# A hybrid decoder layer on one core: the first layer norm's weight on VectorE, its bias as a 49th extra row

## The chip, the cores and the metric

The kernel runs on one core of a Trainium2 chip. A core has TensorE (PE) for matrix products, VectorE (DVE), ScalarE (ACT) and GpSimd (POOL) for elementwise work, and SyncE (SP), whose queue issues the DMAs of this kernel. The time is that of one execution on the device in microseconds (us); of several executions the median is given. A profile is one further execution, taken with the hardware profiler.

## What is computed

One layer on 2048 prompt tokens, 16 meta tokens and 32 sample tokens (8 sequences of 4). The model width D is 1024. Each token is first layer-normed with a weight and a bias (`ln0_g`, `ln0_b`); the result is both what the projections read and the residual that comes back in the last layer norm.

```python
def layer_norm(x, g, b):
    mu = jnp.mean(xf, -1, keepdims=True)
    var = jnp.mean(jnp.square(xf - mu), -1, keepdims=True)
    return (xf - mu) * lax.rsqrt(var + LN_EPS) * g + b

hp = layer_norm(concat([meta, x_prompt]), ln0_g, ln0_b)
hs = layer_norm(x_sample, ln0_g, ln0_b)
mq, mk, mv, mo, mz, mi, mf, aq, ak, av, az = split_proj(hp @ w_in + b_in)
h_m, state = mlstm_prompt(mq, mk, mv, mi, mf)      # chunks of 128 tokens, one after the other
h_a = swa_prompt(aq, ak, av, sink)                 # window of 128 tokens, the meta tokens always seen
mix = concat([gated_norm(h_m, mo, mz), h_a * silu(az)]) @ w_out
y = layer_norm(2**0.25 * hp + mix, ln_g, ln_b)
```

`mq`, `mk`, `mv`, `mo` have 512 columns each, the gates `mi` and `mf` 4 each, `mz`, `aq` and `az` 512 each, `ak` and `av` 128 each. The sample tokens go through the same layer from cached state; states and key/value caches are outputs too.

## The kernel before

**Tiling.** The prompt is cut into 16 chunks of 128 tokens, one token to a partition. The 32 sample tokens and the 16 meta tokens are the 48 "extra rows" (`NE`), one tile `xe`.

**Precision.** A number is carried as two float16 parts, high and low. A projection of a chunk (`proj`, lines 292 to 297) is 24 matmuls of 128x128 by 128x512 into one PSUM tile `pj`: for each of eight slices of D the high part of x times the high and the low part of w (lines 294 and 295), then the low part of x times the high part of w (line 297). `prep` makes the two parts of a weight: it finds the largest absolute value (`all_max` brings it to all partitions with a matmul, line 135), derives a power of two from it, then scales and rounds on ACT (line 269) and takes the difference on DVE (line 272). The float32 weights come through staging buffers (`stg`, and `stage` in the pool of weights). The extra rows' projection `proj_e` holds the high parts of the 48 rows in partitions 0 to 47 and the low parts from 64 on, so that one pass of 16 matmuls (lines 303 and 304) does both; two DVE operations (lines 307 and 313) add them and the bias.

**Stage A** (`a_steps`) goes through the chunks in order, for q, k, v, o and the gates of the mLSTM. `norm_x` normalises a chunk: `bn_stats` on DVE, the power -0.5 on POOL (line 325), scale and shift by the row's own statistics on ACT (line 331), the multiplication by `gs` and the addition of `bs`, each in two halves, on POOL (lines 374 and 375). Then ACT writes the high part `hl[:, 0]` (line 390) and DVE the low part (line 391), a DMA transposes both to `xT`, and the normalised chunk and `xT` are stored to DRAM (`h_d`, `xT_d`) for stage B. `a_gate` computes the gates; `log_sigmoid_rows` (lines 465 to 477) is a chain of tiny operations, of 128 or 48 partitions by 4 elements, which ends in `Gf` and `Gi`; these are transposed on PE (lines 577 for the extra rows, 739 for chunks). `m_rows`, `m_weights`, `m_T`, `m_S`, `m_num`, `m_kv` are the recurrence (lines 746 to 749 the scans, 823 the state's update). v goes to `vaug`, two tiles, used in turn by even and odd chunks. A bias tile `bA[i]` is `b_in` on all partitions; the evictions of PSUM (lines 423 and 426) add it.

**The start.** The order there is written out. The first chunk is normalised on DVE as a whole (`ln0_first`), is transposed in float32 on PE to `xf`, and its gates, q and k are projected from the float32 weights (`proj32`, line 410: two matmul rows of the trace for each of the eight slices), so that they need not wait for `prep`. v and o of the first chunk take the float16 path, with the transposed `xT0`. Between them stand the projections of the extra rows (`qe`, `ge`, `ke`, `ve`, `oe`), stored to `e_d` for the decode work.

**Extra work.** Sample tokens' work and the preparation of stage B's weights (`jobs`) are steps that are taken in turn with those of `a_steps`.

**Stage B** goes through the chunks once more: aq, ak and av, az, mz, the windowed attention (`s_unit`, `s_pv`), then `b_out`: `o_load` brings the chunk back from `h_d` to a tile `z` of the tag `xs` (two buffers), `o_half` multiplies by `w_out` and adds to `z` (line 1318), and `final` is the last layer norm (lines 1143 to 1145: one pass on DVE, two on POOL).

**Order.** The program is traced in this order, and the tile framework's scheduler then lays down one order for each engine from priorities and a modelled time; each engine executes its own list in order. `dma` holds SP's DMAs behind an anchor. SP's queue is in order too: a DMA that waits for a tile holds those behind it.

## Time and profile before

| what | value |
|---|---|
| time, median of 3 runs | 1107.26 us (1106.24 to 1110.84) |
| the profiled execution | 1109.82 us |
| its span on the core | 1108.0 us |
| mean granted clock of TensorE | 0.976 |
| DVE busy | 771.8 us |
| ACT busy | 411.5 us |

The span is what the profile covers; the 1.8 us around it belong to the execution. "Busy" is the time in which an engine executes something, register, branch, semaphore and DMA-issuing instructions aside. In a table of groups each row has the line, engine, operation, out<-in with the tile names and shapes, the count, then busy us and mean ns of one, then the idle us of the engine just before them with what ended that idle time. In the order of time a row starts with the start and the length in us. In a list of waits, a row says which engine waited, at which tile and line, for what: us in total, times, the longest.

### The profile page before, as it was taken

Reading aid. Unit: us, or ns where it says so; the run is one execution under the profiler, and the core shown is the slowest. Engines: PE = TensorE matmul, PEld = TensorE weight load, DVE = VectorE, ACT = ScalarE, POOL = GpSimd, SP = SyncE. Lnnn points to the kernel's source line nnn. Section 1 sums busy time; section 2 is a strip of 40 time slices with the busy share of each in tenths; the row PEclk is TensorE's granted clock in tenths of the full one; section 3 lists DMA queues with packets and bytes.
Section 4 is the critical chain, followed back from the end, with each engine's and each line's share of the span. In section 5 each row is a group of like instructions: output and inputs, shape, how many; then the busy total and the mean of one; then the engine's idle time right before and its main releaser. Section 6 shows DMA issues by size and latency. Waiting matters only on the chain.

```text
span 1108.0 us, 17830 instructions
## 1 busy us (share of the span) xinstructions
PE 1037.6 (94%) x6471; PEld 576.3 (52%) x6471; DVE 771.8 (70%) x2164; ACT 411.5 (37%) x980; POOL 326.7 (29%) x334
## 2 busy tenths in 40 slices
PE   7569999999898989989999899999999999999996
PEld 3235565655555445546655455555555555555543
DVE  6799677776488798875646766656766565676674
ACT  5653222226134355422214433433443343344430
POOL 4134444323043032321102223333322333332322
PEclk9869999999999999989999999999999999999998
DMA  9735745354773878763296456455454545555442
GB/s 321 200 99 162 148 127 146 101 143 146 202 205 93 253 240 271 219 195 87 58 362 133 105 120 134 119 122 120 109 122 122 138 113 122 126 107 119 100 112 74
DMA packets 246097, 166.03 MB, mean 150 GB/s; under 512 B 207977, under 2 KB 220985, under 8 KB 244441
## 3 DMA queue, kind: packets, MB, share of 16 engines
q1 hardware_dynamic: 246010, 164.90, 57.3%
q8 instruction: 51, 0.84, 0.3%
q14 instruction: 36, 0.29, 0.1%
HBM read 70.32 MB, written 45.68 MB: 105 GB/s over the span
## 4 chain that ended last, share of the span: by engine, by line
PE 68%; DVE 12%; DMA 11%; issue 4%; ACT 2%; POOL 1%; SPq 1%; DVEq 0%; POOLq 0%; ACTq 0%
PE pj L1314 14%; PE pj L297 14%; PE pj L295 13%; PE pj L294 13%; DMA xT<-hl 4%; PE pt L1234 2%; DMA xs<-in_dram 2%; PE po L1287 2%; DMA stg<-hl 2%; DMA stg<-in_dram 1%; PE pt L758 1%; DVE hl L391 1%; PE po L822 1%; DVE ls L473 1%; PE pj L410 1%
## 5 line engine op out<-in xcount | busy, mean ns | idle before, releaser
L1314 PE MATMUL pj<-wr_o,EE 128*128 128x512 f16 x720 | 167.1, 381 | 2.7 <-DMA EE<-stg 2.4
L295 PEld LDWEIGHTS <-xT 128*128 128x128 f16 x1008 | 99.2, 98 | 99.2 <-issue 6.1
L297 PEld LDWEIGHTS <-xT 128*128 128x128 f16 x1008 | 98.4, 98 | 98.2 <-issue 0.3
L294 PEld LDWEIGHTS <-xT 128*128 128x128 f16 x1008 | 99.4, 99 | 95.6 <-issue 3.6
L1314 PEld LDWEIGHTS <-EE 128*128 128x128 f16 x720 | 70.5, 98 | 79.8 <-DMA EE<-stg 3.3
L1247 POOL TENSOR_TENSOR mhl<-g,mhl 128x32 f16<-128x32 f32 x32 | 18.8, 587 | 144.6 <-ACT mhl L1246 140.2
L1247 POOL TENSOR_TENSOR mhl<-SI,mhl 128x32 f16<-128x32 f32 x32 | 19.0, 592 | 137.2 <-ACT mhl L1246 137.2
L1243 DVE TENSOR_TENSOR hl<-g,hl 128x512 f16<-128x512 f32 (+1 forms) x32 | 23.2, 724 | 40.7 <-ACT hl L1242 40.7
L294 PE MATMUL pj<-w_v,xT 128*128 128x512 f16 x128 | 50.1, 391 | 0.0
L295 PE MATMUL pj<-w_v,xT 128*128 128x512 f16 x128 | 49.7, 388 | 0.4 <-DVE w_v L272 0.4
L294 PE MATMUL pj<-w_k,xT 128*128 128x512 f16 x120 | 47.0, 391 | 2.1 <-DVE cols L123 1.1
L374 POOL TENSOR_TENSOR xs<-xs,gb 128x512 f32<-128x512 f32 (+1 forms) x32 | 43.5, 1380 | 18.0 <-ACT xs L331 18.0
L1241 ACT ACTIVATE g<-g,nb 128x272 f32<-128x272 f32 (+1 forms) x64 | 32.4, 506 | 43.9 <-DVE nb L1238 43.9
L783 POOL TENSOR_TENSOR qs<-qs,SI 128x512 f32<-128x512 f32 x16 | 21.5, 1343 | 91.9 <-ACT SI L774 91.9
L295 PE MATMUL pj<-w_o,xT 128*128 128x512 f16 x128 | 48.5, 379 | 0.0
L294 PE MATMUL pj<-wr_az,xT 128*128 128x512 f16 x128 | 48.5, 379 | 0.0
L294 PE MATMUL pj<-w_o,xT 128*128 128x512 f16 x128 | 48.5, 379 | 0.0
L294 PE MATMUL pj<-wr_aq,xT 128*128 128x512 f16 x128 | 48.5, 379 | 0.0
L295 PE MATMUL pj<-wr_aq,xT 128*128 128x512 f16 x128 | 48.5, 379 | 0.0
L295 PE MATMUL pj<-wr_az,xT 128*128 128x512 f16 x128 | 48.5, 379 | 0.0
L294 PE MATMUL pj<-wr_z,xT 128*128 128x512 f16 x128 | 48.5, 379 | 0.0
L295 PE MATMUL pj<-wr_z,xT 128*128 128x512 f16 x128 | 48.5, 379 | 0.0
(451 smaller groups left out, 2549.2 us busy)
## 6 DMA issues: line engine op xcount, KB each, us to landing
stg<-in_dram SPq DMA_DIRECT2D x28, 512.0 KB
xs<-in_dram SPq DMA_DIRECT2D x16, 512.0 KB
h_d<-xs SPq DMA_DIRECT2D x16, 512.0 KB
xT_d<-xT SPq DMA_DIRECT2D x16, 512.0 KB
xs<-h_d SPq DMA_DIRECT2D x16, 512.0 KB
xT<-xT_d SPq DMA_DIRECT2D x16, 512.0 KB
out_dram<-xs SPq DMA_DIRECT2D x15, 512.0 KB
hn_d<-g SPq DMA_DIRECT2D x16, 258.0 KB
```

Source lines behind the costliest of these rows:

```text
L294: T.matmul(ps, xT[:, k, :], w.t[:, k, 0, :n], start=(k == 0), stop=False)
L295: T.matmul(ps, xT[:, k, :], w.t[:, k, 1, :n], start=False, stop=False)
L297: T.matmul(ps, xT[:, KT + k, :], w.t[:, k, 0, :n], start=False, stop=(k == KT - 1))
L374: G.tensor_tensor(x[:, c], x[:, c], gs[:rows, c], op=ALU.mult)
L391: V.scalar_tensor_tensor(hl[:, 1], xs, s_x, hl[:, 0], op0=ALU.mult, op1=ALU.subtract)
L783: G.tensor_tensor(c.qs, c.qs, c.SI, op=ALU.mult)
L1234: T.matmul(ps[:, lo:], c.qT[:, h], kTs[:, 2 * (h // 4) + x, lo:], start=(x == 0), stop=(x == 1))
L1241: A.activation(p[:, i, lo:], p[:, i, lo:], AF.Exp, bias=nb[:, h:h + 1], accum_out=sums[:, h:h + 1])
L1243: V.tensor_tensor(hl[:, 1, 2 * q:2 * q + 2, lo:], p[:, :, lo:2 * P], hl[:, 0, 2 * q:2 * q + 2, lo:], op=ALU.subtract)
L1247: G.tensor_tensor(m[:, 1], p[:, :, 2 * P:], m[:, 0], op=ALU.subtract)
L1287: T.matmul(pso[:, h], l, r, start=False, stop=(i == len(last) - 1), skip_group_check=True)
L1314: T.matmul(ps, c.yT[:, a, :], w[:, k, t, :], start=(first and j == 0), stop=(last and j == len(mm) - 1))
```

## The change

The normalised row is (x - mu) * rs * g + b, with rs the reciprocal deviation of the row. The changed kernel keeps (x - mu) * g in the tile and in `h_d`, puts rs into the scale with which the float16 parts are made (`rx`), and leaves b out of what the projections read. In its place b itself becomes row 49 of the extra rows (`NB`), and each projection of that row gives b times the weights plus `b_in`: the bias that all chunks need. It is sent to DRAM and broadcast back into `bA[i]`, `bg2` and stage B's bias tiles. Stage B makes z * rs + b when it has loaded a chunk, with all rs kept in `rss`, and with b broadcast into `lb0`, which lies in the two `vaug` halves, now one tile. The first chunk's exact normalised form is put in a tile of its own, `h`, for the float32 path, and its v and o come from the float32 weights, ahead of their `prep`. `ln0_` of the extra rows is two DVE operations.

```diff
-    def proj_e(out, E, w, n, bias, t1, rows=NE, ps=None):
+    def proj_e(out, E, w, n, bias, t1, rows=NB, ps=None):
...
-    def layer_norm_stats(x, rows, eps, tag):
+    def layer_norm_stats(x, rows, eps, tag, rs=None):
...
-    def normalise(x, rows, mv, rs, tag):
-        mr = small(f"mr_{tag}", 1)[:rows]
-        V.scalar_tensor_tensor(mr, mv[:, 0:1], -1.0, rs, op0=ALU.mult, op1=ALU.mult)
-        A.activation(x, x, AF.Identity, scale=rs, bias=mr)
...
     def ln0_first(x):
-        mv, rs = layer_norm_stats(x, P, EPS, "a")
+        h = work("xT", [P, D])
+        mv, rs = layer_norm_stats(x, P, EPS, "a", rss[:, 0:1])
...
-        last = V.scalar_tensor_tensor(x, x, rs, bs, op0=ALU.mult, op1=ALU.add)
+        V.scalar_tensor_tensor(h, x, rs, bs, op0=ALU.mult, op1=ALU.add)
...
     def ln0_(x, rows):
         mv, rs = layer_norm_stats(x, rows, EPS, "a")
-        normalise(x, rows, mv, rs, "a")
-        for i in range(2):
-            c = slice(512 * i, 512 * i + 512)
-            G.tensor_tensor(x[:, c], x[:, c], gs[:rows, c], op=ALU.mult)
-            G.tensor_tensor(x[:, c], x[:, c], bs[:rows, c], op=ALU.add)
+        V.scalar_tensor_tensor(x, x, mv[:, 0:1], gs[:rows], op0=ALU.subtract, op1=ALU.mult)
+        V.scalar_tensor_tensor(x, x, rs, bs[:rows], op0=ALU.mult, op1=ALU.add)
...
     def norm_x(n, xs):
-        ln0_(xs, P)
+        mv, rs = layer_norm_stats(xs, P, EPS, "a", rss[:, n:n + 1])
+        rx = small("rx", 1)
+        V.tensor_scalar(rx, rs, s_x, None, op0=ALU.mult)
+        V.scalar_tensor_tensor(xs, xs, mv[:, 0:1], gs, op0=ALU.subtract, op1=ALU.mult)
         hl = work("hl", [P, 2, D], F16)
-        A.activation(hl[:, 0], xs, AF.Copy, scale=s_x)
-        V.scalar_tensor_tensor(hl[:, 1], xs, s_x, hl[:, 0], op0=ALU.mult, op1=ALU.subtract)
+        A.activation(hl[:, 0], xs, AF.Copy, scale=rx)
+        V.scalar_tensor_tensor(hl[:, 1], xs, rx, hl[:, 0], op0=ALU.mult, op1=ALU.subtract)
...
+    vaug2 = cst.tile([P, 2 * H * 129], F32, name="vaug")
+    vaug = [vaug2[:, 516 * i:516 * i + 516].rearrange("p (h d) -> p h d", d=129) for i in range(2)]
...
+    def new_bias(i):
+        dma(bA[i], e_d[NE:NB, i].partition_broadcast(P))
...
     last = proj_e(qe, ET, wA[0], 512, bA[0], t1)
     dma(e_d[:, 0], qe)
+    new_bias(0)
...
+    dma(g_d, ge[NE:NB])
+    dma(bg2, g_d.partition_broadcast(P))
+    log_sigmoid_rows(ge[:NE], NE, 1)
...
+    a_proj(0, 2, stv)
     wA[2] = prep("v", stv, 512, sums=(0,1,2))
-    a_proj(0, 2)
     last = proj_e(ke, ET, wA[1], 512, bA[1], t1)
     dma(e_d[:, 1], ke)
+    new_bias(1)
+    a_proj(0, 3, sto)
     xTs[1] = norm_x(1, x1)
     wA[3] = prep("o", sto, 512, sums=range(4))
-    a_proj(0, 3)
     last = proj_e(ve[:, :, 0:P], ET, wA[2], 512, bA[2], t1)
     dma(e_d[:, 2].rearrange("t (h d) -> t h d", d=P), ve[:, :, 0:P])
+    new_bias(2)
...
     dma(e_d[:, 3], oe)
+    new_bias(3)
...
-        proj_e(E.z[:NE], ET, w, 512, e_bias(E.eb, 3336, 512), E.t1)
+        proj_e(E.z[:NB], ET, w, 512, e_bias(E.eb, 3336, 512), E.t1)
+        dma(b_d[:, 1024:1536], E.z[NE:NB])
...
-    bq, bkv, baz, bz = bias_tile(2568, 512), bias_tile(3080, 256), bias_tile(3336, 512), bias_tile(2048, 512)
+    bq, bkv, baz, bz = (bias_tile(o, n, src=b_d) for o, n in ((512, 512), (0, 256), (1024, 512), (1536, 512)))
+    lb0 = vaug2[:, 0:D]
+    dma(lb0, ln0[1:2, :].partition_broadcast(P))
...
     def o_load(n):
         c = cb[n]
         c.z = work("xs", [P, D])
         dma(c.z, h_d[n])
+        V.scalar_tensor_tensor(c.z, c.z, rss[:, n:n + 1], lb0, op0=ALU.mult, op1=ALU.add)
```

Stage B's other three projections of the extra rows get their row 49 and their store to `b_d` in the same way.

More of the change, by code (lines that the diff above doesn't have):

```diff
@@ L189, in tile_hymba_step @@
     load(stq, w_a[0])
-    xe = work("xs", [P, D])[:NE]
+    xb = work("xs", [P, D])[:NB]
+    xe = xb[:NE]
     first(xe, x_e)
+    first(xb[NE:NB], ln0[1:2, :])
     stk = stage(512, "w")
@@ L211, in tile_hymba_step @@
     Gi = [cst.tile([P, P], F32, name=f"Gi{i}") for i in range(2)]
-    vaug = [cst.tile([P, H, 129], F32, name=f"vaug{i}") for i in range(2)]
+    vaug2 = cst.tile([P, 2 * H * 129], F32, name="vaug")
+    vaug = [vaug2[:, 516 * i:516 * i + 516].rearrange("p (h d) -> p h d", d=129) for i in range(2)]
+    rss = cst.tile([P, NCH], F32, name="rss")
     EE = work("EE", [P, 2, D], F16)
@@ L224, in tile_hymba_step @@
     he_d = dr.tile([NE, D], F32, name="he_d")
-    e_d = dr.tile([NE, 4, 512], F32, name="e_d")
+    e_d = dr.tile([NB, 4, 512], F32, name="e_d")
+    g_d = dr.tile([1, 8], F32, name="g_d")
+    b_d = dr.tile([1, 2048], F32, name="b_d")
     hne_d = dr.tile([NS, 512], F32, name="hne_d")
@@ L550, in tile_hymba_step @@
     ln0_(xe, NE)
-    split_e(EE[:, 0], xe, NE, s_x)
+    split_e(EE[:, 0], xb, NB, s_x)
     dmat(ET, EE[:, 0])
@@ L574, in tile_hymba_step @@
     last = proj_e(ge, ET, wg, 8, bg, t1, ps=pt)
-    log_sigmoid_rows(ge, NE, 1)
+    bg2 = cst.tile([P, 8], F32, name="bg2")
+    dma(g_d, ge[NE:NB])
+    dma(bg2, g_d.partition_broadcast(P))
+    log_sigmoid_rows(ge[:NE], NE, 1)
     pr = pt([P, 2, P])
@@ L846, in e_bias @@
     def e_bias(t, off, n):
[L847 removed]
+        dma(t[:NB, :n], b_in[0:1, off:off + n].partition_broadcast(NB))
         return t[:, :n]
```

49 lines of the change are left out of this document (27 added, 22 removed).

## The prediction

> **What bounds the kernel now.** I read the page's busy table and its slices first, then tables of whole stretches, then the waits of TensorE (PE), then the order of time on single engines.
>
> ```profile
> span 1108.0 us, 17830 instructions
> PE 1037.6 (94%) x6471; PEld 576.3 (52%) x6471; DVE 771.8 (70%) x2164; ACT 411.5 (37%) x980; POOL 326.7 (29%) x334
> PE   7569999999898989989999899999999999999996
> ```
>
> PE is busy 94% of the span; 1108.0 - 1037.6 = 70.4 us are all that it idles. Where it never idles, only less PE work would help. So the question is which stretches hold the 70 us, and the slices point at the first 110 us (four slices of 27.7 us). The table by stretch splits it (columns: stretch, then busy us of PE, weight loads, DVE, ACT, POOL, the granted clock, DMA share, GB/s):
>
> ```profile
> 600.00:1060.00 460.00, 454.95 (x3005) 247.13 (x3004) 296.43 (x829) 181.22 (x534) 141.59 (x159) 1.00 0.54 119
> 40.50:113.40 72.90, 46.52 (x232) 23.98 (x229) 66.06 (x171) 35.49 (x57) 27.50 (x25) 0.79 0.51 137
> 113.40:500.00 386.60, 366.35 (x2273) 210.48 (x2274) 294.63 (x823) 135.00 (x249) 118.37 (x97) 0.98 0.63 177
> ```
>
> In the second stage (600 to 1060) PE idles 5.0 us of 460, while DVE idles 163.6. In the first stage after its start (113 to 500 of it) PE idles 20.3 of 386.6. From 40.5 to 113.4 it idles 26.4 of 72.9 and runs at a granted clock of 0.79, while DVE is busy 66.06 of 72.9, or 91%: here DVE is the bound. The waits of PE between 40 and 114 us name the places:
>
> ```profile
> PE px L303 <- DVE qs L313: 12.6, 1, 12.6
> PE pt L577 <- DVE Gf L476: 7.4, 1, 7.4
> PE pt L739 <- DVE Gf L476: 3.9, 1, 3.9
> ```
>
> The last two wait for the gates, a dozen operations on tiny tiles. Beside them stands GpSimd (POOL), which scales and shifts chunks 1 and 2:
>
> ```profile
> 56.27 4.93 POOL L374 TENSOR_TENSOR xs<-xs,gb 128x512 f32<-128x512 f32 x4
> 61.17 4.91 POOL L375 TENSOR_TENSOR xs<-xs,gb 128x512 f32<-128x512 f32 x4
> ...
> 60.04 1.19 DVE L470 TENSOR_TENSOR ls<-ls 48x4 f32<-48x4 f32 x1
> 61.26 1.19 DVE L471 TENSOR_SCALAR ls<-ls 48x4 f32<-48x4 f32 x1
> 62.49 3.99 DVE L473 SCALAR_TENSOR_TENSOR ls<-ls 48x4 f32<-48x4 f32 x5
> ...
> 530.61 0.16 DVE L470 TENSOR_TENSOR ls<-ls 128x4 f32<-128x4 f32 x1
> 530.81 0.17 DVE L471 TENSOR_SCALAR ls<-ls 128x4 f32<-128x4 f32 x1
> 531.01 0.95 DVE L473 SCALAR_TENSOR_TENSOR ls<-ls 128x4 f32<-128x4 f32 x5
> ```
>
> L470 and L471 take 0.16 and 0.17 us at 530, with POOL quiet, and five of L473 0.95; beside POOL the first two take 1.19 each, about the length of one POOL operation (4.93 / 4 = 1.23), and the five 3.99. So POOL's normalisation holds DVE up, and PE behind it. That is the theory on which the forecast stands.
>
> **The change, part by part.** The sum is made against the profiled execution's own 1109.8 us (span 1108.0 and 1.8 around it); the median of the runs shown is 1107.3, 2.6 lower. The forecast puts the sum on that median.
>
> *POOL's part goes.* L374 and L375 leave POOL: 64 operations, for 15 chunks and the 48 extra rows; with them goes ACT's pass L331, on an engine busy 37%, at no gain. What they cost DVE in the stretch from 40.5 to 113.4 is read from the groups of DVE there:
>
> ```profile
> L473 DVE SCALAR_TENSOR_TENSOR ls<-ls 128x4 f32<-128x4 f32 (+1 forms) x14 | 8.3, 594 | 0.3
> ...
> L471 DVE TENSOR_SCALAR ls<-ls 48x4 f32<-48x4 f32 (+1 forms) x2 | 2.5, 1232 | 0.1
> L476 DVE SCALAR_TENSOR_TENSOR Gf<-ls 128x4 f32<-128x4 f32 (+1 forms) x3 | 2.0, 663 | 0.0
> L470 DVE TENSOR_TENSOR ls<-ls 48x4 f32<-48x4 f32 (+1 forms) x2 | 1.3, 674 | 0.0
> ...
> L469 DVE TENSOR_TENSOR ls<-ls 48x4 f32<-48x4 f32 (+1 forms) x2 | 1.1, 570 | 0.1
> L467 DVE TENSOR_SCALAR ls<-ls 48x4 f32<-48x4 f32 (+1 forms) x2 | 1.1, 554 | 0.2 <-ACT ls L466 0.2
> ```
>
> At 0.95 / 5 = 0.19 us each, 14 of L473 would take 2.7 (5.6 saved). At 0.16 each, L471, L470, L469 and L467 would take 0.3 (2.2, 1.0, 0.8 and 0.8 saved) and three of L476 0.5 (1.5 saved). Together 11.9 us of DVE time.
>
> *DVE's new work in stage A.* Each chunk gets one scalar_tensor_tensor of 128x1024 in f32 in norm_x, for a small one that goes (mr) and a small one that comes (rx). Its nearest row is the first chunk's:
>
> ```profile
> 16.52 1.27 DVE L363 SCALAR_TENSOR_TENSOR xs<-xs,rs_a,gb 128x1024 f32<-128x1024 f32 x1
> ...
> L391 DVE SCALAR_TENSOR_TENSOR hl<-xs,cols,hl 128x1024 f16<-128x1024 f32 x15 | 20.9, 1394 | 16.8 <-ACT hl L390 16.8
> ```
>
> I take 1.27; 1.39 is the upper end, with POOL's share in it. Chunks 1 to 3 fall into the stretch: +3.8. DVE's floor there becomes 66.1 - 11.9 + 3.8 = 58.0 us. If DVE stays 91% busy the stretch takes 58.0 / 0.906 = 64.0, a gain of 8.9; filled to the last it takes 58.0, a gain of 14.9. The 48 rows' own two passes (ln0_) fall at about 17 us, in place of an ACT pass and POOL's four: their 2 x 1.27 bound a loss of 2.5; they stand ahead of split_e, and the first weights' load covers them. I take nothing.
>
> *v and o of chunk 0 in float32.* They need the staged weights and nothing of prep, so PE may run them in the 12.6 us in which it now waits for qs (o's first, if v's have not landed). Cost, from q's and k's in the chain that ended last, and from v's f16 form in the order of time:
>
> ```profile
> 20.23 8.96 PE pj L410 x20
> ```
>
> ```profile
> 82.90 0.38 PE L295 MATMUL pj<-w_v,xT 128*128 128x512 f16 x1
> 83.11 1.89 PE L297 MATMUL pj<-w_v,xT 128*128 128x512 f16 x8
> ```
>
> 20 steps take 8.96, 0.448 each; a projection has 16 (two for each of eight k), or 7.2. The f16 form takes 24 steps of (1.89 - 0.38) / 7 = 0.216, or 5.2 (0.38 is one matmul's own length, and the next one starts 0.21 after it). So PE is given 2 x 2.0 = 4.0 us of work more, but 10.4 us of f16 work leave the second half of the stretch for that wait. PE's floor in the stretch is then 46.5 + 4.0 = 50.5, less cold running (clock 0.79): below DVE's 58.0. PE does not set it, DVE does. I take **-12** for the stretch, the middle of 8.9 and 14.9.
>
> *The rest of stage A.* DVE gets 12 x 1.27 = 15.2 us on 294.6 in 386.6, 80%, before the stalls that POOL no longer causes. Of PE's 20.3 idle us some are such stalls; the order of time on PE shows two that begin beside L374 or L375:
>
> ```profile
> 190.18 1.16 PE L758 MATMUL pt<-rM,sel 128*128 128x128 f32 x8 [1.54 <-DVE rM L749]
> ...
> 414.24 1.16 PE L758 MATMUL pt<-rM,sel 128*128 128x128 f32 x8 [1.70 <-DVE rM L749]
> ```
>
> I take **-3**, these two. The ends: -8 (two fifths of the 20.3), and +8, half of the new 15.2 uncovered.
>
> *Stage B's new pass.* o_load gets z*rs + b: 16 x 1.27 = 20.3 us on DVE. Its cover is DVE's idle 163.6; in each chunk two gaps hold it:
>
> ```profile
> L1243 DVE TENSOR_TENSOR hl<-g,hl 128x512 f16<-128x512 f32 x28 | 19.4, 692 | 38.0 <-ACT hl L1242 38.0
> ...
> L1190 DVE SCALAR_TENSOR_TENSOR qT<-pj,cols,bias 128x512 f32<-128x512 f32 x7 | 5.3, 751 | 21.5 <-PE pj L297 21.5
> ```
>
> L1190 waits 3.1 a chunk, L1243 1.4 an instruction. I take **+0.5**, and **+0.5** for the tail, where PE waits on DVE anyway; ends 0 and 20.3.
>
> *Biases by way of DRAM.* Row 49 of each extra-row projection is stored, then broadcast into bA; on SP each broadcast waits for its store, and the first evictions of chunk 1 wait for the broadcasts. The rows around it:
>
> ```profile
> 40.25 5.78 DMA he_d<-xs
> ...
> 88.11 6.31 DMA xs<-in_dram
> ```
>
> ```profile
> 53.18 0.33 SPq L103 DMA_DIRECT2D e_d<-qs  x1
> ```
>
> ```profile
> 92.23 0.38 PE L294 MATMUL pj<-w_q,xT 128*128 128x512 f16 x1
> ```
>
> The trace has no such pair. Bounded above by the two long transfers one after the other, 5.8 + 6.3 = 12.1 us; below by 0: the store of q's rows leaves at 53.2, so its broadcast is there by 65.3, and chunk 1's q starts at 92.2 now, so not before 77.3 if the whole 14.9 is gained. Queued behind the broadcast on SP is chunk 1's transpose xT<-hl, and behind an eviction that waits for bA stand all later ones on DVE. I take nothing for the four and the gates' bg2, which goes the same way early on; o's, the last, has the least cover, and the 12.1 stay as an end. In stage B the four biases come from b_d in place of b_in, with as many transfers, and their stores are long done: nothing. lb0 waits until vaug is read for the last time, and stands in SP's queue ahead of sink_t and stage B's loads, whose buffers come free at the same place; I take nothing, with the same 6.3 as an end.
>
> Sum: -12 - 3 + 0.5 + 0.5 = -14 on 1109.8, or 1095.8; on the median 1107.3 - 14 = 1093.3. Forecast **1093**, or 1.3% faster.
>
> **Rivals.**
>
> *The start stays as it is (no change).* Every instruction's place on its engine is laid down anew by the scheduler, and if v and o push the extra rows' k back, or new passes land ahead of the gates, DVE's released time isn't used. Then the two gate waits shrink by half (5.7) and half of PE's 4.0 is paid: -3.7, giving 1104. For it: DVE is 91% busy already. Against it: the two gate waits sit right behind POOL.
>
> *Stage B pays (slower).* The new pass stands in DVE's order and waits for z's load; behind it stand the evictions that free PE's two pj buffers. Price, from the waits of DVE for such loads in stage A, and from a scaling pass of POOL in stage B:
>
> ```profile
> DVE st_a L319 <- DMA xs<-in_dram: 19.8, 11, 3.5
> ...
> L1144 POOL TENSOR_TENSOR xs<-xs,gb 128x1024 f32<-128x1024 f32 x13 | 30.6, 2354 | 12.1 <-DVE xs L1143 12.1
> ```
>
> A wait of 19.8 / 11 = 1.8 and the pass of 1.27 are 3.1 a chunk, 49 over 16. It decides once more than 15 of the 49, the gain of the first stage, reach PE, 1 us a chunk; at two thirds it is +33: 1107.3 - 15 + 33 = 1125. Against it: the two gaps above are 3.1 and 1.4. A longer price would be 2.35 of POOL on top, if the stalls of the first stage came back here; 16 x 2.35 = 38 more, on DVE.
>
> The Trainium skill speaks for that longer price: "SBUF — State Buffer", section "Who interferes with whom", says that a DVE instruction with two SBUF inputs and a GpSimd instruction that reads SBUF exclude each other for the whole instruction. The new pass has two such inputs, so by that rule it may be held for one of L1144 or L1145, or hold them; the sum would then be the longer price. DVE's idle 163.6 holds that too, so it changes the sum only where this rival comes true. The stalls beside L374 agree with the rule for L470 and L473, which read two tiles; L471 reads one and is held all the same.
>
> *The change doesn't keep its double buffer (slower).* vaug's two halves become one tile; if a write of one half had to wait for the readers of the other, v's eviction would wait for m_kv of the chunk before. The trace shows both:
>
> ```profile
> 538.99 0.75 DVE L423 SCALAR_TENSOR_TENSOR vaug<-pj,cols,bias 128x512 f32<-128x512 f32 x1
> ...
> 543.22 0.60 DVE L823 SCALAR_TENSOR_TENSOR Cst<-Cst,dec,po 128x129 f32<-128x129 f32 x2
> ```
>
> Held until there, the eviction is 4.2 us late, 63 over 15 chunks; with half of it covered by the second pj buffer, 1107.3 - 15 + 31 = 1123. Against it: the kernel keeps all its scales as columns of one tile, cols, and every engine works on other columns at the same time.
>
> *PE sets the start after all.* If DVE's list were shorter than I count, PE's floor of 50.5 would give -22.4, and with -8 in the rest of stage A and +1 in B 1078.
>
> **How the numbers follow.** Forecast 0.63 (1083 to 1100), PE-bound start 0.06, no change 0.17, stage B 0.10, double buffer 0.04. The range 1083 to 1110 leaves out about 0.06 below and 0.14 above. A measurement of this kernel tells 0.5%, 5.5 us, from no change: faster than 1101.7 is the forecast, the PE-bound start and about 0.04 of the no-change case, 0.73; slower than 1112.8 is 0.13; 0.14 lies between.
>
> **What would show it.** Between 40 and 70 us PE should hold 32 more f32 matmuls in a row where it idled 12.6, the wait of L577's successor for Gf should be under 1 us, and L473's group should mean near 0.16. The stretch up to the first chunk's gates (113.4) should end 10 to 15 us earlier with DVE at over 90%. In stage B, PE's idle should stay near 5 us of 460 and the new pass should cost 1.3. It is wrong if tiny DVE operations still take 1.2 us, if PE waits for bA, or if evictions in stage B start late behind the new pass.

## The result, and the profile after

The changed kernel takes **1177.28 us** (median of 4 runs, 1174.94 to 1178.64) against 1108.72 for the kernel before (median of the 4 runs beside them): a ratio of **1.0617**, 95% interval 1.0586 to 1.0648. It is 69 us slower; forecast were 14 us faster. The times of the runs below are medians that leave out two executions far above all others of their kernel (1822 us in `pass_in_a`, 3152 us in `before_one_vaug`). The page of the changed kernel, its span and the busy shares, then the costliest group that the kernel before does not have:

```profile
span 1176.9 us, 17745 instructions
PE 1061.9 (90%) x6455; PEld 582.2 (49%) x6455; DVE 767.5 (65%) x2197; ACT 392.4 (33%) x964; POOL 253.0 (21%) x270
...
L1333 DVE SCALAR_TENSOR_TENSOR xs<-xs,rss,vaug 128x1024 f32<-128x1024 f32 x16 | 20.5, 1284 | 68.2 <-DMA xs<-h_d 68.2
```

POOL lost 73.7 us of work (326.7 to 253.0), as the change meant, and DVE did not gain any to speak of. But PE now idles 1176.9 - 1061.9 = 115.0 us in place of 70.4. The table by stretch of the changed kernel (columns as before) says where; the first two stretches are those shown of before, the third is stage B:

```profile
40.50:113.40 72.90, 57.23 (x244) 27.23 (x243) 58.15 (x179) 32.63 (x59) 12.06 (x9) 0.87 0.70 197
113.40:500.00 386.60, 352.01 (x2174) 203.90 (x2173) 267.86 (x797) 118.49 (x230) 62.75 (x48) 0.96 0.59 165
...
640.00:1100.00 460.00, 421.86 (x2715) 224.21 (x2715) 278.42 (x753) 161.47 (x476) 127.10 (x143) 0.99 0.46 107
```

PE's idle in the first stretch went from 26.4 to 15.7, as hoped. In the rest of stage A it grew from 20.3 to 34.6 of 386.6, and in 460 us of stage B from 5.0 to 38.1. The marks between the stages are the first and the last eviction of aq in the order of time of DVE, first of the kernel before:

```profile
577.54 0.75 DVE L1160 SCALAR_TENSOR_TENSOR q<-pj,cols,bias 128x512 f32<-128x512 f32 x1 [3.29 <-PE pj L297]
...
1045.12 0.74 DVE L1160 SCALAR_TENSOR_TENSOR q<-pj,cols,bias 128x512 f32<-128x512 f32 x1
```

and of the changed kernel:

```profile
600.13 0.75 DVE L1184 SCALAR_TENSOR_TENSOR q<-pj,cols,bias 128x512 f32<-128x512 f32 x1 [3.29 <-PE pj L304]
...
1114.71 0.75 DVE L1184 SCALAR_TENSOR_TENSOR q<-pj,cols,bias 128x512 f32<-128x512 f32 x1
```

Stage B starts 22.6 us later, and its chunks take 514.6 us in place of 467.6, 47.0 more; the end behind them takes 0.7 less. That is the whole loss. These two numbers, called **the start of B** and **the length of B** below, are read from each run.

**Stage B.** The waits of PE in the changed kernel from 640 to 1100 us:

```profile
PE po L1311 <- DMA stg<-hl: 14.5, 11, 2.4
PE pj L301 <- DVE xs L1343: 10.6, 9, 1.6
PE pj L1339 <- DMA EE<-stg: 7.5, 1, 7.5
```

None names the new pass L1333. It stands one step further back, in the waits of DVE in the same stretch:

```profile
DVE xs L1333 <- DMA xs<-h_d: 61.0, 12, 6.8
```

and in the order of time of DVE, beside that of SP:

```profile
897.83 1.28 DVE L1333 SCALAR_TENSOR_TENSOR xs<-xs,rss,vaug 128x1024 f32<-128x1024 f32 x1 [4.56 <-DMA xs<-h_d]
899.03 0.69 DVE L1267 TENSOR_TENSOR hl<-g,hl 128x512 f16<-128x512 f32 x1
899.63 0.75 DVE L1225 SCALAR_TENSOR_TENSOR qs<-pj,cols,bias 128x512 f32<-128x512 f32 x1
```

```profile
890.70 0.96 SPq L104 DMA_DIRECT2D out_dram<-xs  x1
894.12 0.32 SPq L104 DMA_DIRECT2D xs<-h_d  x1
```

The load goes out at 894.12, as soon as the store of an older chunk has left the buffer, and the pass stands in DVE's list right behind it. DVE stops 4.56 us for it; behind it wait L1267, which feeds the transposed probabilities that PE's L1311 needs, and L1225, an eviction that frees a `pj` buffer. Counted through, this is the ninth pass, chunk 8's, while the next two additions (903.14 and 912.25) are chunk 7's: chunk 8's comes at 938.53. The pass waits at once for data that are wanted 40 us later.

**Stage A.** When the gates of some chunks are ready (start of the last operation, L476 before and L481 after, us):

| chunk | 1 | 2 | 3 | 5 | 6 | 8 | 9 | 10 | 15 |
|---|---|---|---|---|---|---|---|---|---|
| before | 111.7 | 141.3 | 180.6 | 246.7 | 289.0 | 352.4 | 408.6 | 438.8 | 550.4 |
| after | 118.9 | 143.7 | 167.2 | 231.4 | 287.4 | 351.7 | 424.7 | 459.9 | 573.0 |

Chunks 3 and 5 are 13 and 15 us early, chunk 4 (202.2 against 207.0) only 5, and chunk 1, whose gates were forecast 10 to 15 us earlier, is 7 us late. At chunk 6 little is left of the gain; from 8 to 9 the kernel takes 73.0 us where it took 56.2. There PE stops once for long, at the maximum of `w_z`, one of the weights for stage B that the side jobs (`jobs`) prepare:

```profile
403.21 0.79 PE L136 MATMUL pt<-dg,ones 128*128 128x128 f32 x2 [12.39 <-DVE dg L135]
```

DVE could not give the maximum earlier, since SP issued the loads of `w_z` only at 388.91, behind `wd_az`, the store of the weight before it. In the order of time of SP, changed kernel:

```profile
378.80 0.61 SPq L104 DMA_DIRECT2D ea<-o_d  x2
379.52 0.34 SPq L104 DMA_DIRECT2D o_d<-xa  x1
379.90 5.00 SPq L104 DMA_DIRECT2D ea<-o_d  x14
388.53 0.34 SPq L104 DMA_DIRECT2D wd_az<-w_az  x1
388.91 3.99 SPq L104 DMA_DIRECT2D stg<-in_dram  x4
```

and the kernel before:

```profile
352.76 0.35 SPq L103 DMA_DIRECT2D o_d<-xa  x1
353.15 5.67 SPq L103 DMA_DIRECT2D ea<-o_d  x14
...
362.81 0.35 SPq L103 DMA_DIRECT2D wd_az<-w_az  x1
363.21 2.67 SPq L103 DMA_DIRECT2D stg<-in_dram  x3
```

The chunks were early and the side jobs 26 us late. So two theories go into the experiments: stage B pays for a wait and not for work; and in stage A a chain of side jobs, not the chunks' own start, sets the end, and one part of the change made that chain late. Both are argued from the traces so far, and not yet shown.

### The profile page after: what moved, and what is told of

Read it like the earlier page. It is cut to its first block, busy times and chain, and to the rows that moved or that the text cites. A ratio compares the mean times of both kernels' runs of the same rounds, so it can differ in the third digit from the quotient of the medians.

```text
span 1176.9 us, 17745 instructions
## 1 busy us (share of the span) xinstructions
PE 1061.9 (90%) x6455; PEld 582.2 (49%) x6455; DVE 767.5 (65%) x2197; ACT 392.4 (33%) x964; POOL 253.0 (21%) x270
## 4 chain that ended last, share of the span: by engine, by line
PE 35%; DMA 29%; DVE 22%; ACT 5%; issue 4%; POOL 3%; SPq 1%; DVEq 0%; ACTq 0%; POOLq 0%
PE pj L301 8%; PE pj L302 8%; PE pj L304 7%; DMA stg<-hl 7%; DMA xs<-h_d 4%; DMA out_dram<-xs 3%; DVE hl L1267 3%; PE pj L1339 3%; DMA stg<-in_dram 3%; DMA xs<-in_dram 2%; DVE g L1259 2%; DMA At<-hn_d 1%; SPq L104 1%; ACT g L1265 1%; ACT SI L1265 1%
## 5 line engine op out<-in xcount | busy, mean ns | idle before, releaser
L1339 PE MATMUL pj<-wr_o,EE 128*128 128x512 f16 x720 | 167.2, 387 | 7.6 <-DMA EE<-stg 7.5
L302 PEld LDWEIGHTS <-xT 128*128 128x128 f16 x992 | 98.3, 99 | 120.0 <-issue 30.8
L301 PEld LDWEIGHTS <-xT 128*128 128x128 f16 x992 | 98.5, 99 | 103.3 <-issue 7.4
L304 PEld LDWEIGHTS <-xT 128*128 128x128 f16 x992 | 96.0, 98 | 96.6
L1333 DVE SCALAR_TENSOR_TENSOR xs<-xs,rss,vaug 128x1024 f32<-128x1024 f32 x16 | 20.5, 1284 | 68.2 <-DMA xs<-h_d 68.2
L333 POOL TENSOR_TENSOR rss<-ve_a,mhalf 128x1 f32<-128x1 f32 x16 | 25.2, 1574 | 138.0 <-DVE ve_a L330 106.7
L301 PE MATMUL pj<-w_q,xT 128*128 128x512 f16 x120 | 46.5, 387 | 4.8 <-DMA xT<-hl 4.3
L1265 ACT ACTIVATE SI<-SI,nb 128x272 f32<-128x272 f32 (+1 forms) x64 | 32.4, 507 | 49.9 <-DVE nb L1262 49.9
L800 POOL TENSOR_TENSOR qs<-qT 128x512 f32<-128x512 f16 x16 | 21.2, 1322 | 122.7 <-PE po L825 61.6
L301 PE MATMUL pj<-w_v,xT 128*128 128x512 f16 x120 | 47.0, 392 | 0.0
L302 PE MATMUL pj<-w_v,xT 128*128 128x512 f16 x120 | 46.8, 390 | 0.0
```

The source lines that it names most:

```text
L301: T.matmul(ps, xT[:, k, :], w.t[:, k, 0, :n], start=(k == 0), stop=False)
L302: T.matmul(ps, xT[:, k, :], w.t[:, k, 1, :n], start=False, stop=False)
L304: T.matmul(ps, xT[:, KT + k, :], w.t[:, k, 0, :n], start=False, stop=(k == KT - 1))
L333: G.tensor_tensor(rs, ve, mhalf[:rows, 0:1], op=ALU.pow)
L800: G.tensor_tensor(c.qs, c.qT[:, 0], c.qT[:, 1], op=ALU.add)
L1265: A.activation(p[:, i, lo:], p[:, i, lo:], AF.Exp, bias=nb[:, h:h + 1], accum_out=sums[:, h:h + 1])
```

## The experiments

A time is the median of two to ten executions, with its ratio to the kernel before, run beside it; the marks are read from one profile of each run. "x_kv" and "x_q" are the evictions of these side jobs' projections (L313, L314 or L320 by the kernel), "wd_az" the issue of that store, all in us.

| run | time | ratio, interval | x_kv | x_q | wd_az | start of B | length of B |
|---|---|---|---|---|---|---|---|
| before (profile) | 1107 to 1110 | 1 | 253.4 | 277.6 | 362.8 | 577.5 | 467.6 |
| after | 1177.3 | 1.0617, 1.0586 to 1.0648 | 258.5 | 294.5 | 388.5 | 600.1 | 514.6 |
| pass_in_a | 1145.6 | 1.0330, 1.0283 to 1.0378 | 263.9 | 303.9 | 398.0 | 608.8 | 473.5 |
| pass_late | 1137.9 | 1.0240, 1.0215 to 1.0264 | 259.6 | 295.9 | 390.0 | 601.8 | 474.6 |
| f16_vo | 1165.8 | 1.0513, 1.0455 to 1.0571 | 257.6 | 284.1 | 361.5 | 579.5 | 520.0 |
| f16_vo_pass_late | 1113.6 | 1.0034, 1.0010 to 1.0059 | 253.4 | 280.1 | 356.7 | 580.0 | 471.9 |
| before_dve_ln | 1113.1 | 1.0043, 1.0019 to 1.0066 | 253.2 | 278.8 | 361.7 | 579.0 | 470.6 |
| before_one_vaug | 1103.9 | 0.9947, 0.9922 to 0.9972 | 250.8 | 275.5 | 361.8 | 571.6 | 468.0 |
| before_f32_vo | 1136.3 | 1.0247, 1.0198 to 1.0297 | 254.7 | 292.9 | 389.1 | 599.9 | 469.2 |
| before_f32_v | 1128.1 | 1.0178, 1.0118 to 1.0237 | 267.0 | 292.8 | 379.2 | 596.3 | 468.2 |
| before_f32_o | 1121.1 | 1.0114, 1.0061 to 1.0168 | 260.2 | 286.6 | 371.3 | 587.3 | 467.9 |
| f32_vo_pace | 1169.6 | 1.0535, 1.0501 to 1.0569 | 262.7 | 284.5 | 370.1 | 633.8 | 469.5 |
| before_pace | 1148.7 | 1.0347, 1.0303 to 1.0390 | 252.7 | 274.6 | 355.3 | 613.0 | 469.0 |
| f32_vo_pace6 | 1134.8 | 1.0238, 1.0184 to 1.0291 | 255.6 | 292.9 | 372.7 | 603.4 | 469.4 |
| f32_vo_burst_act | 1131.6 | 1.0213, 1.0163 to 1.0263 | 257.4 | 303.5 | 384.6 | 601.0 | 471.0 |
| before_burst_act | 1128.9 | 1.0188, 1.0172 to 1.0205 | 253.2 | 305.7 | 383.6 | 596.1 | 467.7 |
| f16_late_burst_act | 1132.4 | 1.0221, 1.0193 to 1.0248 | 252.4 | 302.1 | 383.1 | 599.0 | 471.7 |
| f32_vo_side_first | 1116.9 | 1.0080, 1.0052 to 1.0108 | 254.0 | 289.8 | 370.3 | 580.7 | 468.7 |
| before_side_first | 1113.6 | 1.0036, 1.0019 to 1.0053 | 253.2 | 287.5 | 369.3 | 579.7 | 469.0 |
| after_both_mended | 1122.1 | 1.0100, 1.0068 to 1.0132 | 256.8 | 291.4 | 374.8 | 586.5 | 472.1 |

### Stage B: the pass taken out, and the pass put later

`pass_in_a` finishes the normalisation in stage A; it also has no `lb0`, and stores the first chunk's `h` in place of its `x`:

```diff
         V.scalar_tensor_tensor(hl[:, 1], xs, rx, hl[:, 0], op0=ALU.mult, op1=ALU.subtract)
+        V.scalar_tensor_tensor(xs, xs, rs, bs, op0=ALU.mult, op1=ALU.add)
...
     def o_load(n):
-        V.scalar_tensor_tensor(c.z, c.z, rss[:, n:n + 1], lb0, op0=ALU.mult, op1=ALU.add)
```

> The changed kernel, but z*rs+b is done by VectorE in the first stage, right behind the f16 split, and the finished rows are stored; the second stage loads them and has no pass and no lb0. Theory (the pass stands in VectorE's order and waits for z's load, which has only two buffers): the second stage, from the first aq eviction to the last, falls from 514.6 us back to within 3 of before's 467.6, and the total from 1177 to about 1130; the first stage keeps its loss, the last gates standing at about 573 + up to 10 for 12 uncovered passes. Rival (the second stage lost by its biases from b_d, by lb0 or by the vaug tile, or by an order laid anew): it stays above 500 and the total above 1165.

The length of B fell to 473.5, 5.9 over the kernel before where the theory allowed 3, and far from the rival's 500; the total came out at 1146 and not 1130, because stage A lost 8.7 more. So the pass, or its place, makes the loss of stage B. Which of the two, `pass_late` tells: it keeps the pass and the load, and only forbids it to stand ahead of the z gate's eviction of the chunk that is worked on beside it.

```diff
+        c.zm = V.scalar_tensor_tensor(zm, ps, wB["z"].ev, bz, op0=ALU.mult, op1=ALU.add).ins
...
-    def o_load(n):
+    def o_load(n, after=None):
...
-        V.scalar_tensor_tensor(c.z, c.z, rss[:, n:n + 1], lb0, op0=ALU.mult, op1=ALU.add)
...
+        with tc.issue_after(after):
+            V.scalar_tensor_tensor(c.z, c.z, rss[:, n:n + 1], lb0, **p)
...
     def b_out(n):
-        o_load(n)
+        o_load(n, cb[n + 1].zm)
```

> The changed kernel, but in the chunks of the second stage's loop z*rs+b may stand in VectorE's order only behind the eviction of the z gate (L1225), some ten instructions ahead of the o_add that needs it, and no longer right behind the load for the chunk after. The first stage's orders are untouched. Theory (what costs is the wait for the load in VectorE's order, 14 waits of 4 to 5 us, not the 1.28 us of the pass): the waits for xs<-h_d are gone, the second stage from first to last aq eviction takes 470 to 490 us in place of 514.6, total 1133 to 1153. Rival (the pass itself has no cover and costs its length and more wherever it stands): 500 or more, total above 1162.

The length of B is 474.6, 40.0 less than in the changed kernel, with the same 16 passes. The groups of the pass (L1338 in the loop, L1335 for three chunks at the end) and two rows from the order of time, in this run:

```profile
L1338 DVE SCALAR_TENSOR_TENSOR xs<-xs,rss,vaug 128x1024 f32<-128x1024 f32 x13 | 16.6, 1275 | 0.0
...
L1335 DVE SCALAR_TENSOR_TENSOR xs<-xs,rss,vaug 128x1024 f32<-128x1024 f32 x3 | 3.9, 1286 | 10.6 <-DMA xs<-h_d 10.6
```

```profile
904.47 0.74 DVE L1225 SCALAR_TENSOR_TENSOR qs<-pj,cols,bias 128x512 f32<-128x512 f32 x1
905.14 1.27 DVE L1338 SCALAR_TENSOR_TENSOR xs<-xs,rss,vaug 128x1024 f32<-128x1024 f32 x1
910.10 0.75 DVE L1348 SCALAR_TENSOR_TENSOR xs<-pj,cols,xs 128x512 f32<-128x512 f32 x1 [0.83 <-PE pj L1344]
```

Thirteen passes have no idle before them. With all 16 passes the length of B is 7.0 over that of the kernel before (474.6 - 467.6), and only 1.1 over that of `pass_in_a`, which has no pass there; most of the 7.0 is thus not the pass's, and what makes it is not shown (`before_dve_ln` below, whose stage B is that of the kernel before, has 470.6). The place of the pass in the order cost 40.0. This settles stage B: **the wait was the price, not the pass.**

### Stage A: the parts of the change one by one

`before_dve_ln` puts only the layer norm of the kernel before on DVE, with two passes a chunk and no bias route:

```diff
     def ln0_(x, rows):
-        normalise(x, rows, mv, rs, "a")
-        for i in range(2):
-            c = slice(512 * i, 512 * i + 512)
-            G.tensor_tensor(x[:, c], x[:, c], gs[:rows, c], op=ALU.mult)
-            G.tensor_tensor(x[:, c], x[:, c], bs[:rows, c], op=ALU.add)
+        V.scalar_tensor_tensor(x, x, mv[:, 0:1], gs[:rows], op0=ALU.subtract, op1=ALU.mult)
+        V.scalar_tensor_tensor(x, x, rs, bs[:rows], op0=ALU.mult, op1=ALU.add)
```

> The kernel before with one part alone: the first layer norm's scale and shift move from ScalarE and GpSimd to two VectorE passes a chunk, both in the first stage; biases, v, o and the second stage as before. Theory (GpSimd's passes hold VectorE up in the start; taking them away brings the start's gain of some 10 to 15 us, and twelve later chunks cost up to 15 us of uncovered passes): chunk 3's gates at 125 to 135 in place of 141.3, total 1090 to 1110. Rival (the loss in the middle of the first stage comes from VectorE's new passes themselves): the 192 us from chunk 5's to chunk 10's gates become over 215 here too, total above 1125.

The 141.3 in that text are chunk 2's gates by the numbering here; they came at 146.3, later. The total fits the theory's range at its upper end (1113.1, 0.4% slower), but its reason fails: of the start's gain nothing reached stage B, which began at 579.0. Chunk 1's gates came at 105.1 in place of 111.7, and those of chunks 3 and 5 were 7.5 us early, but at chunk 6 nothing was left (289.2 against 289.0). The tiny operations did get short. The group of L470 (L473 in the kernel before, 594 ns there) from 40.5 to 113.4 us:

```profile
L470 DVE SCALAR_TENSOR_TENSOR ls<-ls 128x4 f32<-128x4 f32 (+1 forms) x15 | 2.3, 156 | 0.3
```

And yet that stretch is no better for PE, which waits 24.7 of 72.9 us there (26.4 before), only elsewhere:

```profile
40.50:113.40 72.90, 48.16 (x246) 25.29 (x245) 64.54 (x187) 31.36 (x53) 13.28 (x9) 0.74 0.55 159
```

```profile
PE pt L574 <- DVE Gf L473: 8.4, 1, 8.4
PE pt L612 <- DVE ea L603: 6.5, 1, 6.5
PE px L303 <- ACT w_k L269: 4.9, 1, 4.9
PE px L304 <- DVE w_k L272: 2.9, 3, 1.7
```

The wait of 12.6 us for `qs` is gone, and the same chain waits for the parts of `w_k` and for the gates instead. DVE is as full as ever, 64.5 us of 72.9: the freed time was taken by work from further down its list.

`f16_vo` (the changed kernel with v and o of chunk 0 from f16 weights again) and `before_f32_vo` (the kernel before with float32 v and o alone) isolate the third part. `f16_vo` also issues the first chunk's transpose `xT0` ahead of its store to `h_d`. The edit of `before_f32_vo`, which `f16_vo` undoes:

```diff
+    a_proj(0, 2, stv)
     wA[2] = prep("v", stv, 512, sums=(0,1,2))
-    a_proj(0, 2)
...
+    a_proj(0, 3, sto)
     xTs[1] = norm_x(1, x1)
     wA[3] = prep("o", sto, 512, sums=range(4))
-    a_proj(0, 3)
```

> The changed kernel, but chunk 0's v and o come from the f16 weights again, after their preparation, as before. Theory (the float32 matmuls ahead of w_q's maximum push the weights' loads and splits back, and with them the whole order of the first stage): the gates of chunk 1 come at about 112 again (118.9 in the changed kernel), and the 73 us between chunk 8's and chunk 9's gates shrink towards 56; total 1150 to 1165. Rival (the loss between chunks 5 and 10 has another cause, such as the extra passes on VectorE or the bias route): those 73 us stay within 5, and the total stays at 1170 to 1185. The second stage stays at about 514 by both.

> The kernel before with one part of the change alone: chunk 0's v and o from float32 weights. Theory (that part costs what chunk 1's late gates show, and may upset the order of the first stage): 1107 to 1140, with chunk 1's gates later than 111.7. Rival (by itself it fills the wait for the gates, as the forecast had it): 1095 to 1105. The second stage stays at 467.6 within 3 by both.

Both theories held in stage A. Without the float32 form the changed kernel's stage B starts at 579.5 in place of 600.1, with 52.8 us from chunk 8 to 9; with the form alone the kernel before shows the changed kernel's picture to the chunk: gates of 3 and 5 early (162.6 and 227.0), 6 at 285.1, 74.6 us from 8 to 9, start of B at 599.9. `f16_vo` came at 1165.8, just outside the theory's range, since its stage B is longer (520.0). Both losses taken out together, in `f16_vo_pass_late`:

> The changed kernel with both suspected costs taken out: chunk 0's v and o from f16 weights, and z*rs+b held behind L1225 in VectorE's order. What is left of the change is the layer norm on VectorE and the bias by way of the 49th row. Theory (the two account for all of the loss): first aq eviction at 577 to 583, the second stage 470 to 478 us, total 1108 to 1120. Rival (the bias route or lb0 cost something of their own): total above 1125.

1113.6 us, as the theory had it: of the 69 us, 64 are these two. What stays is the layer norm on DVE and the bias route, together 0.3% slower than the kernel before, about what `before_dve_ln` costs without the bias route. The route itself shows one wait, that of chunk 1's v for its bias in the changed kernel:

```profile
DVE vaug L428 <- DMA bias<-e_d: 3.7, 1, 3.7
```

`before_one_vaug` makes the two `vaug` tiles one and changes no operation.

> The kernel before, with the two vaug tiles made halves of one tile and nothing else: the same instructions and the same dependences. Theory (the order that is laid is the same or nearly, and no double buffer is lost): 1105 to 1112. Rival A (a lost double buffer): v's evictions late, above 1115. Rival B (any small edit lays the first stage's order anew, with jumps of 10 us and more): the gates of chunks 5 to 10 move by over 10 us against before with no operation changed, either way.

No double buffer is lost, and the order does not jump by this edit: 1103.9, with all gates within 6 us. That a small edit lays the order anew by chance, with a jump of 22 us, is not seen here; one edit does not exclude it.

### Why float32 v and o cost 22 us

By the forecast's estimate they need 4 us more of PE. PE's table by stretch, kernel before:

```profile
150.00:260.00 110.00, 108.31 (x708) 64.68 (x709) 80.60 (x236) 32.05 (x64) 46.02 (x38) 1.00 0.49 137
260.00:580.00 320.00, 301.85 (x1858) 172.44 (x1856) 234.32 (x661) 113.44 (x216) 69.29 (x58) 0.98 0.64 190
```

and `before_f32_vo`:

```profile
150.00:260.00 110.00, 110.00 (x713) 64.64 (x712) 72.89 (x226) 28.08 (x57) 40.15 (x33) 1.00 0.49 132
260.00:580.00 320.00, 280.87 (x1690) 161.41 (x1689) 224.84 (x634) 111.72 (x208) 65.57 (x56) 0.95 0.57 165
```

From 150 to 260 PE is full in both. Gates that are 20 us earlier there are not time won: x_kv comes at 254.7 against 253.4, so the early chunks were paid for by the side jobs. After 260 PE idles 39.1 of 320 us in place of 18.2, and that is the loss. The first idea was the place in SP's order, where the float32 form has a transpose `xT<-hl` ahead of the transfers `ea<-o_d`. Runs that take side jobs' steps earlier in the program:

```diff
-        for _ in a_steps(n):
-            for _ in range(1):
+        for j, _ in enumerate(a_steps(n)):
+            for _ in range(2 if 1 <= n <= 5 and j % 3 == 0 else 1):
                 next(extra, None)
```

> The kernel before with v and o of chunk 0 from float32 weights, and the steps of the side jobs (sample tokens, preparing the second stage's weights) taken twice at every third step of chunks 1 to 5, so that they stand about a third earlier beside these chunks. Theory (the chunks of the first stage run ahead early and then wait beside the side jobs, whose chain sets the end of the stage): x_q's eviction comes earlier than 292.9, and the first aq eviction earlier than 599.9 by 10 to 22; total 1112 to 1128. Rival (the chunks' own work sets it): first aq eviction within 4 of 599.9 or later, total 1133 or more.

> The control to the run on the side jobs' pace: the kernel before with the same doubled steps and nothing else. Theory (here the chunks themselves are late at the start, so that side jobs taken earlier only stand in their way or change nothing): first aq eviction 575 to 590, total 1105 to 1120. Rival (the side jobs bound the stage here too): earlier than 572, total below 1102.

Both theories failed. x_q came early (284.5 and 274.6), but then the chunks stalled: 110.9 and 96.8 us from chunk 3's gates to chunk 4's. PE idles 19.9 and 15.2 us of these, 12.0 and 11.1 of it in one wait for a weight's maximum, and works for the rest. Stage B started 34 and 36 us later; how the stall grew to that is not shown. A milder form, double steps only at every other step of chunk 6:

> The kernel before with v and o of chunk 0 from float32 weights, and side jobs taken twice at every other step of chunk 6 alone, some five steps. In SyncE's laid order the second transpose xT<-hl that the float32 form has ahead of the transfers ea<-o_d is then behind them, and wd_z and wd_o come one chunk earlier. Theory (the 22 us of the first stage come from that place in the order: the side jobs' weights are late and the chunks wait for them from chunk 8 to 9): those 74.6 us shrink below 62 and the first aq eviction comes at 574 to 588 in place of 599.9, total 1110 to 1125. Rival (the loss comes from chunk 0's extra 4 us of PE work and the later extra rows, and passes through whatever the order): first aq eviction within 5 of 599.9, total 1131 to 1140.

It failed as well: wd_az came at 372.7 in place of 389.1, but the stall moved from chunk 8 to chunk 7 (92.7 us from 7 to 8). Then each half of the float32 form by itself, whose order in SP is that of the kernel before at that place:

> The kernel before with chunk 0's v alone from float32 weights. SyncE's laid order around the transfers ea<-o_d and the weights' stores is that of the kernel before. Theory (the order, not the work, makes the loss): first aq eviction 570 to 585, total 1100 to 1115. Rival (each float32 projection costs half of the 22 us): first aq eviction 586 to 592, total about 1120.

> The kernel before with chunk 0's o alone from float32 weights; the laid order of SyncE in the middle is again that of the kernel before. Theory: first aq eviction 570 to 585, total 1100 to 1115. Rival: first aq eviction 586 to 592, total about 1120.

Again the theory failed; the rival's number holds for o (587.3, 1121.1), and v costs more (596.3, 1128.1). Each alone makes the side jobs late from the first: x_kv at 267.0 and 260.2 against 253.4. The order of time of PE shows how the wait for `qs` was filled. With both, in `before_f32_vo`, it is filled much as the forecast had it: 24 of the 32 matmul rows stand in it, and PE waits 2.92 us. But the other eight stand ahead of the pass with `w_q` from which `qs` comes, and the first matmul with `w_k` comes 5.0 us later than in the kernel before (53.21):

```profile
44.72 3.68 PE L410 MATMUL pj<-stg,SI 128*128 128x512 f32 x8
...
58.19 0.39 PE L303 MATMUL px<-w_k,EE 128*128 128x512 f16 x1 [2.92 <-DVE qs L313]
```

In `before_f32_o` o's matmuls were not laid into the wait:

```profile
52.66 0.61 PE L303 MATMUL px<-w_k,EE 128*128 128x512 f16 x1 [12.09 <-DVE qs L313]
...
73.31 4.74 PE L410 MATMUL pj<-stage,wt 128*128 128x512 f32 x8
```

v's alone shorten the wait and set its end back as well; first the kernel before, then `before_f32_v`:

```profile
53.21 0.61 PE L303 MATMUL px<-w_k,EE 128*128 128x512 f16 x1 [12.56 <-DVE qs L313]
```

```profile
44.75 3.68 PE L410 MATMUL pj<-stg,SI 128*128 128x512 f32 x8
57.47 0.61 PE L303 MATMUL px<-w_k,EE 128*128 128x512 f16 x1 [9.04 <-DVE qs L313]
```

The side jobs themselves were then handled in two ways. First, 32 small transfers of x_kv on ACT's queue in place of SP's:

```diff
-                    dma(Vm[i][r:r + NM, :, h], vd[NS:NE, i])
+                    A.dma_start(out=Vm[i][r:r + NM, :, h], in_=vd[NS:NE, i])
...
-                dma(dst[b, 140:144, :], E.kvx[4 * b:4 * b + 4, i * P:(i + 1) * P])
+                A.dma_start(out=dst[b, 140:144, :], in_=E.kvx[4 * b:4 * b + 4, i * P:(i + 1) * P])
```

> The kernel before with chunk 0's v and o from float32 weights, and the 32 small transfers of the side job x_kv (16 into Vm, 16 rows of the caches) issued from ScalarE's queue and no longer from SyncE's. Theory (with the float32 form a transpose that still waits for its data stands ahead of these transfers and of wd_aq in SyncE's one queue, and the side jobs lose 14 us there between x_kv's and x_q's evictions): the 38 us between these two become 22 to 30, the first aq eviction comes 8 to 20 earlier than 599.9, total 1113 to 1127. Rival (the side jobs are late by VectorE's and TensorE's orders, not by SyncE's queue): the 38 us stay above 34 and the first aq eviction within 5 of 599.9.

> The control: the kernel before with the same 32 transfers on ScalarE's queue. Theory (they hold SyncE's queue in the kernel before too, some 15 us with the transposes behind them, but the idle of TensorE from 260 to 300 us is only 2.6): total 1100 to 1110. Rival (ScalarE's own work is held up by waiting for the transfers' data): above 1112.

> The version that might beat both: the changed kernel with v and o from f16 weights, z*rs+b held behind L1225 in VectorE's order, and the 32 small transfers of x_kv on ScalarE's queue. Theory (each of the losses is out and SyncE's queue is freer): 1098 to 1110. Rival (the start's gain is not to be had, since TensorE is filled from 150 to 260 us whatever the start does): 1108 to 1118.

All three theories missed: the first by x_q, which came later still (303.5); the control at 1128.9, where its rival had it; the third at 1132.4, 19 slower than `f16_vo_pass_late`. The order of time of ACT in `before_burst_act`:

```profile
260.45 11.54 ACTq L875 DMA_DIRECT2D Vm<-vd  x16
272.03 4.64 ACTq L884 DMA_DIRECT2D out_dram<-ea  x13
276.71 1.06 ACT L255 ACTIVATE w_aq<-stg 128x1024 f16<-128x1024 f32 x1 [21.35 <-DMA out_dram<-ea]
```

ACT spent 16 us on issuing, and `w_aq`, the next weight, began 19.8 us later than before (256.90). The chunks' own work on ACT stood behind the transfers too: the copy of a chunk's transposed gates (L742) came at 283.18 in place of 263.02, and chunk 6's gates at 313.5 in place of 289.0. So side jobs and chunks were delayed together, and that wd_az came 20.8 and stage B 18.6 us later does not tell which of them sets the end. Second, first choice for the side jobs' instructions in the scheduler's reckoning, with no instruction added or removed:

```diff
         for job in (x_kv, x_q, x_swa, x_az, x_z):
-            yield from job()
+            steps = job()
...
+                if job in (x_q, x_swa, x_az):
+                    with tc.high_priority():
+                        more = next(steps, steps) is not steps
```

> The kernel before with chunk 0's v and o from float32 weights, and the instructions of the side jobs x_q, x_swa and x_az given first choice wherever they are ready in the scheduler's reckoning. Theory (the side jobs' chain from x_q to x_az sets the end of the first stage, and stands behind chunk work in VectorE's and TensorE's orders): x_q's eviction earlier than 288, the first aq eviction 582 to 595, total 1113 to 1128. Rival (in the scheduler's reckoning these instructions already stand where their data come ready, so the order hardly changes): first aq eviction 597 to 604, total 1130 to 1140.

1116.9, as the theory had it, with stage B at 580.7, even before the range's lower end; 19 of the 22 us are back. x_q moved less than expected (289.8); most was won behind it, up to wd_az, in SP's order:

```profile
361.10 0.35 SPq L103 DMA_DIRECT2D o_d<-xa  x1
...
370.33 1.44 SPq L103 DMA_DIRECT2D wd_az<-w_az  x1
```

The control, and the same order in the changed kernel with `pass_late`'s:

> The control to f32_vo_side_first: the kernel before with the instructions of x_q, x_swa and x_az given first choice in the scheduler's reckoning, and nothing else. Theory (the float32 form alone pushes the side jobs behind chunk work, and here they already stand where they should): 1104 to 1112, the first aq eviction within 5 of 577.5. Rival (the side jobs bound the first stage here as well): faster than 1100.

> The changed kernel with every part of the change kept, and the two found losses answered by order alone: z*rs+b held behind L1225 in VectorE's order, and x_q, x_swa and x_az given first choice. Theory (the two orders are the loss of the change): 40 us from the second stage and 15 to 22 from the first, so 1113 to 1125 in place of 1177. Rival (the first stage of the changed kernel loses by something else than the float32 form in the kernel before): 1130 or more, as with the held pass alone (1138).

The kernel before gets nothing from it (1113.6, 0.4% slower, 1.6 us over the theory's range); its side jobs came later with first choice than without (x_q at 287.5, wd_az at 369.3). The changed kernel, with every part of the change kept, comes from 1177 to 1122 by order alone, as the theory had it.

Leave out the three paced runs, in which the chunks themselves stalled (wd_az 355.3 to 372.7, start of B 603.4 to 633.8). Then stage B starts at 572 to 581 us wherever wd_az is issued up to 370.3, whether at 356.7 or at 369.3, and 9 to 31 us later than the 577.5 of before where it is issued at 371 to 398. This is read from the runs afterwards, with three of them left out. With `f32_vo_side_first`, where order alone brought wd_az 18.8 and the start of B 19.2 us forward, it speaks for the side jobs' chain as what sets the end of stage A once it is late; no run moves that chain and nothing else. Ahead of that, something else holds 572 to 581.

## Why the prediction was wrong

**POOL's part: the mechanism right, its worth wrong.** The stalls do go: L478 in the changed kernel against L473's 594 ns and 8.3 us before.

```profile
L478 DVE SCALAR_TENSOR_TENSOR ls<-ls 128x4 f32<-128x4 f32 (+1 forms) x10 | 1.5, 147 | 0.1
```

But "if DVE stays 91% busy the stretch takes 64.0" was the wrong step, and so was the sum that carried its gain to the end of the kernel. The same window of time holds other work once the old is shorter, and what counts is when PE's inputs come. In `before_dve_ln` chunk 1's gates came 6.6 us earlier, where 12 were taken, but PE's idle in the stretch fell by only 1.7 us: the gates moved ahead of other work of PE. By chunk 6 nothing was left, and stage B began 1.5 us later than before; forecast were 12 and 3 earlier. The rival "the start stays as it is" described this part, though not by its price.

**v and o in float32: the failing step of stage A.** The forecast let them fill a wait of 12.6 us and counted 4 us of PE work. The filling came true: all 32 matmul rows stand between 43.0 and 59.3 us in the changed kernel. Yet alone v and o cost 22.4 us (start of B in `before_f32_vo`). The wait was on a chain (`qs`, then the parts of `w_k`, then the gates), and work put ahead of the chain's next matmul on an engine with an order of its own delays the chain: 5.0 us at `w_k`'s first matmul in `before_f32_vo`, 3.7 at chunk 1's gates. The gain at chunks 3 to 5, which did come, lay ahead of 110 us in which PE is full. The rest of the 22.4 arises behind them, where the chunks wait and the side jobs are late. The forecast read 20.3 us of PE idle in the rest of stage A as room for small gains. It never asked what the side jobs wait for, and its upper end of +8 for that stage was far too small.

**DVE's new pass in stage A** was sized right: forecast 1.27, and in the changed kernel

```profile
L393 DVE SCALAR_TENSOR_TENSOR xs<-xs,mv_a,gb 128x1024 f32<-128x1024 f32 x15 | 19.1, 1271 | 0.0
```

**Stage B's new pass: the other failing step.** "I take +0.5", since DVE's gaps cover 1.27 us; it was +47.0. The gaps were there: `pass_late`, with all 16 passes, is 1.1 longer than `pass_in_a` with none. What failed is the assumption that the pass stands in a gap: in an order laid by a modelled time it stood behind a load that on the chip needed 3.7 us from issue to pass. The rival "stage B pays" named the mechanism and gave 0.10; its price of 1.8 + 1.27 a chunk was low. The rows show a wait of 61.0 / 12 = 5.1, and the lengthened B is 47.0 / 15 = 3.1 a chunk, by chance the rival's sum. Its point of decision, 15 us reaching PE, was passed, and it would have given 1125 with the start's gain; without that and with stage A's loss the time is 1177.

The longer price, for which the Trainium skill's "SBUF — State Buffer", section "Who interferes with whom", spoke, did not come: it would hold a pass with two SBUF inputs beside POOL's L1168 and L1169. The 16 passes took 1284 ns in the mean, and by the starts and lengths in the order of time none of them, here or in `pass_late`, runs while L1168 or L1169 does. So the rule was not put to a test, and no run here shows it for this pass.

**Biases by way of DRAM**: taken at 0 with an end of 12.1. One wait of 3.7 is there, and `f16_vo_pass_late` against `before_dve_ln` (1113.6 and 1113.1) leaves nothing for the route, lb0 and the pass moved from stage A to B, taken together. **The double buffer** was not lost. **The tail's** +0.5 was -0.7: from the last eviction of aq to the end 62.2 us in place of 62.9.

Open stays what holds the start of B at 572 to 581 when the side jobs are early, and why v's and o's float32 forms delay the side jobs by more alone (at x_kv) than together. No kernel here beats the one before by more than about the 0.5% that a measurement tells; `before_one_vaug`, of which two executions count, is 0.5% faster (0.9922 to 0.9972).
